# A streaming-encoder block on one core: the norm row loaded as one row and spread by two one-row products, and the opening's hand-written order rewritten up to the third tile

## The chip, the core and the metric

The kernel runs on one core of one Trainium2 chip. The core has a matrix engine (PE, whose weight loads the profile lists apart as PEld), a vector engine (DVE), a scalar engine (ACT), a general engine (POOL), and a sync engine (SP), which in this kernel does nothing but issue transfers. Each engine works through its own instructions in their order; an instruction waits for what it needs from other engines, and everything behind it on the same engine waits with it. Transfers run beside the engines.

The metric is the device time of one execution in microseconds (us). Before the change the median of three runs is 1209.71 us.

## The reference, cut to what matters

One block: a mixer with two branches, then a squared-ReLU MLP, for 1024 tokens of width 1024 and 16 meta tokens put ahead of them, all in float32.

```python
def rmsnorm(x, g):
    xf = x.astype(jnp.float32)
    y = xf * lax.rsqrt(jnp.mean(xf * xf, axis=-1, keepdims=True) + EPS)
    return (y * g.astype(jnp.float32)).astype(x.dtype)

def hybrid_mixer(u, w_in, ...):
    z = jnp.einsum('bld,dn->bln', u, w_in)
    a, q, k, v, r, lr, ga, gb = jnp.split(z, IN_SPLITS, axis=-1)
    ...
    return jnp.einsum('bld,de->ble', m, w_out)

def reference(x, meta_tokens, norm_mix, w_in, ...):
    meta = jnp.broadcast_to(meta_tokens[None].astype(x.dtype), (B, N_META, D_MODEL))
    h = jnp.concatenate([meta, x], axis=1)
    for l in range(DEPTH):                                  # DEPTH = 1
        h = h + hybrid_mixer(rmsnorm(h, norm_mix[l]), w_in[l], ...)
        h = h + squared_relu_mlp(rmsnorm(h, norm_ffn[l]), w_ff1[l], w_ff2[l])
    return rmsnorm(h, norm_final)[:, N_META:]
```

The change touches only the first line of the mixer: `rmsnorm(h, norm_mix[l])`, its transposes, and the first part of `u @ w_in`, the columns of `v` (512) and of `lr` (16).

## The kernel before, in words

The block is a row of stages. The change lies in the first, `first_stage`, and in the table `ORDER_1` that orders it. This stage takes the tokens in eight tiles of 128 and a ninth of the 16 meta tokens. For each tile it computes the norm, writes the normed tile, turns it by transposes (the channels must lie on the partitions for the products), and multiplies it with the columns of `w_in` for `v` and `lr`. The turned tiles stay in memory and serve all later stages.

**Precision.** PE multiplies float32 slowly, so nearly all products of the kernel are made with split operands: a matrix is held as a rounded part (`th`, `vw[:, 0]`, type fp32r) and the rest (`tl`, `vw[:, 1]`), and a product is three products (lines 285 to 287). ACT makes a rounded part by a copy, DVE the rest by a subtraction. The one exception is the first result, tile 0 with the first 256 columns: it is made in plain float32 from an unsplit copy `xr` of the turned tile (line 388), which doesn't have to wait for any splitting.

**The words of the order.** `ORDER_1` is a list of words, worked off one after the other when the program is written; ACT, DVE and SP keep this order as it stands (a manual schedule); PE's is left to a scheduler, which here leaves the turns and products in the order of the words. The first digit is the tile, or the number of the column block for words that deal with weights; the second is which half of the 1024 channels.

| word | engine | what it does | line before |
|---|---|---|---|
| `square t` | ACT | squares of the tile, summed per token, into a spare tile `um` | 488 |
| `log t`, `exp t` | ACT | first guess of the inverse root, by way of a logarithm | 491, 494 |
| `root t` | DVE | one Newton step on the guess, 3 small instructions | 498 to 500 |
| `scale t` | DVE | tile times root times norm row `gB`, into `us`; then issues a later tile's load on SP | 504 |
| `turn tj` | PE | 4 transposes 128x128 into a bank, `ms` and `sc` by turns | 519 |
| `keep tj` | ACT | copy of the turned half into `xr` | 525 |
| `hi tj`, `lo tj` | ACT, DVE | rounded part `th` and rest `tl` of the turned half | 532, 535 |
| `high ij`, `low ij` | ACT, DVE | rounded part and rest of weight block i, half j, into `vw`; i = 2 is the small `lr` block | 547, 551 |
| `ask ij` | SP | load of weight block i, half j, into a ring `raw` of two buffers (line 118), so it waits until the old block is used | 461 |
| `value itj` | PE | products of tile t, half j, with weight block i: 4 of plain float32 for the first two words, else 12 split ones | 388, 285 to 287 |
| `out it` | ACT | evacuates a finished result and stores it | 405 |

**Ahead of the words** stands a fixed opening. SP issues the loads of tiles 0 and 1, of the first two weight blocks, of tiles 2 and 3 and of the small `lr` block. ACT's queue issues the load of an identity matrix (`ident`, for the transposes), then the load of the norm row as 8 rows of 128 into eight partitions of a cleared 128x128 corner of `us`, and loads ACT's tables. PE runs two products 128x512 of a cleared buffer whose results nobody reads (`warm(2)`), then spreads the norm row over all partitions: eight products 128x128, each with one column of the identity, repeated, as its other operand, four into each of two banks (line 481). Three more warming products follow (`warm(3)`). DVE copies each of the two banks, times -0.5, into `gB` (line 484); the -0.5 belongs to the Newton step. Only then come the words.

Tile t is held in buffer t mod 4 of `xs`, and normed in buffer t mod 3 of `us`, so a tile's load or its scaling can wait for an earlier tile to be used up.

Of the kernel before, what the change touches and what calls it, by code (L numbers as in the profile page):

```python
# [10 lines left out]
ACT = mybir.ActivationFunctionType  # L11
ALU = mybir.AluOpType
AX = mybir.AxisListType

P = 128
# [3 lines left out]
KT = D // P  # L19
# [103 lines left out]
def kernel(  # L123
# [10 lines left out]
    act, dve, pool, pe = nc.scalar, nc.vector, nc.gpsimd, nc.tensor  # L134
# [19 lines left out]
    def bank(tag):  # L154
        if tag == "sc":
            sc_n[0] += 1
            return two("sc")[:, sc_n[0] % 2]
        return psp[tag].tile([P, 512], F32, name=f"b_{tag}", tag=tag)

    def two(tag):  # L160

        if tag in ("sc", "gs"):
            if tag not in wide:
                wide[tag] = psp[tag].tile([P, 2, 512], F32, name=f"b_{tag}", tag=tag)
            return wide[tag]
        return psp[tag].tile([P, 2, 512], F32, name=f"b_{tag}", tag=tag)
# [204 lines left out]
    def halves():  # L371
        return [slice(h * HALF, (h + 1) * HALF) for h in range(2)]
# [35 lines left out]
    def lr_turn():  # L408
# [13 lines left out]


    ORDER_1 = """
        square0 log0 exp0 root0 square1 scale0 log1 exp1 turn00 high00 root1 turn01 keep00 scale1 keep01 value000
        hi00 low00 ask10 high01 turn10 square2 low01 turn11 value001 ask11 hi10 log2 lo10 exp2 square3 root2 value010 scale2
        hi11 hi01 log3 lo11 out00 turn20 exp3 turn21 hi20 root3 value011 high10 lo20 scale3 high20 hi21 low20 value020 keep10
        keep11 lo01 square4 lo21 turn30 turn31 lo00 hi30 value021 log4 lo30 hi31 keep30 lo31 value030 exp4 keep20 out01
        root4 high11 low10 value031 out02 keep21 square5 scale4 value100 low11 wait00 log5 out03 exp5 turn40 turn41 root5
        value101 hi40 scale5 lo40 hi41 lo41 keep31 keep40 value110 out10 keep41 square6 log6 exp6 value111 value120  # L430
# [8 lines left out]
    def first_stage(xs, us, xm, um, lrraw):  # L439
        xr, vw = S["xr"], S["vw"]  # L440
        vraw = S["vraw"] = []
        x_in = lambda t: xs[:, t % 4] if t < 8 else xm
        x_out = lambda t: us[:, t % 3] if t < 8 else um[:META]
        tok = lambda t: (t // 4, OFF[t // 4] + (t % 4) * P)
        cell = lambda n, t: stat[n][: P if t < 8 else META, t : t + 1]

        def load(t):
            nc.sync.dma_start(xs[:, t % 4], x[t * P : (t + 1) * P, :])
# [2 lines left out]
            return w_in[4 * j * P : 4 * (j + 1) * P, c : c + n].rearrange("(k p) c -> p k c", p=P)  # L451

        blank = xr.rearrange("p k c -> p (k c)")[:, -640:]
        row = us[:, 2, :P]
        nc.scalar.dma_start(ident, ident_in)
        dve.memset(row, 0.0)
        nc.scalar.dma_start(row[:KT], norm_mix.rearrange("(k c) -> k c", c=P))
        act.preload_act_table_set("natural_log_exp_and_others")
        pool.memset(blank, 0.0)
        pool.memset(wgu, 0.0)  # L460
# [11 lines left out]
        def warm(n, cols=HALF):  # L472
            for _ in range(n):
                pe.matmul(bank("ms")[:, :cols], blank[:, HALF:], blank[:, :cols], start=True, stop=True)

        warm(2)
        for h, c in enumerate(halves()):
            b = bank("mm")
            for i in range(4):
                k = 4 * h + i  # L480
                pe.matmul(
                    b[:, i * P : (i + 1) * P], ident[:, k : k + 1].broadcast_to([P, P]), row, start=True, stop=True
                )
            dve.tensor_scalar(gB[:, c], b, -0.5, None, ALU.mult)
        warm(3)

        def square(t):
            act.activation(um[: P if t < 8 else META], x_in(t), ACT.Square, accum_out=cell(3, t))
# [13 lines left out]
        def scale(t):  # L502
            u = x_out(t)
            dve.scalar_tensor_tensor(u, x_in(t), cell(3, t), gB[: u.shape[0]], ALU.mult, ALU.mult)
            if t == 0:
                load(4)
            if t == 1:
                load(5)
                nc.sync.dma_start(xm, meta)
            if t in (2, 3):  # L510
                load(4 + t)

        turned = {}

# [34 lines left out]
        def low(i, j):  # L549
            whole, hi, lo = parts(i, j)  # L550
            dve.tensor_tensor(lo, whole, f32(hi), ALU.subtract)

        does = dict(
            wait=lambda i, j: W1.ask(),
            square=square, log=log, exp=exp, root=root, scale=scale, turn=turn, keep=keep, hi=hi, lo=lo, high=high,
            low=low, ask=ask, value=v_half, out=v_out, first=W1.split, meta=lambda t: transposed(um[:META], 0, 0),
        )
# [1181 lines left out]
```

## Time and profile before

| what | value |
|---|---|
| median of the runs | 1209.71 us |
| single runs | 1208.96, 1209.71, 1209.78 us |
| the profiled execution | 1210.91 us |
| its span (first to last instruction) | 1209.1 us |
| mean granted TensorE clock over it | 0.998 of full speed |
| busy DVE, ACT, POOL | 837.5, 574.4, 79.1 us |
| DMA, mean over the span | 159 GB/s |

The profile shows one execution. A row that begins with two numbers is a run of like instructions that follow each other on an engine: its start and its length in us from the span's start, then the engine, the line, the operation, result <- operands with their shapes, and `x` with the count; in square brackets stands how long the engine was idle just before, and what ended that. Rows of the busy time by stretches begin with start:end. Products on PE are pipelined, so that the length of one is not the distance to the next. The stage of the change takes about the first 74 us of the span; everything behind it is the same code in both kernels.

### The profile page before, as it was taken

What the parts mean: (1) busy time and instruction counts of PE and PEld (TensorE: products, weight loads), DVE (VectorE), ACT (ScalarE), POOL (GpSimd) and SP (SyncE); (2) the same over time, 40 slices, a digit from 0 to 9 for tenths busy, and PEclk for the clock granted to TensorE, in tenths of its full rate; (3) what the DMA queues carried; (4) which work ended last, traced back from release to release, by engine and by line L of the source; (5) the groups of instructions that cost most, each with busy time, mean ns of one, the idle gap of its engine ahead of it and who ended that gap; (6) DMA issues with size and microseconds to landing.
All of it is one profiled execution on the core that took longest, in us unless ns stands there. A gap on an engine that the chain in (4) does not pass through costs nothing.

```text
span 1209.1 us, 18303 instructions
## 1 busy us (share of the span) xinstructions
PE 1194.4 (99%) x6775; PEld 993.1 (82%) x6775; DVE 837.5 (69%) x1369; ACT 574.4 (48%) x1014; POOL 79.1 (7%) x97
## 2 busy tenths in 40 slices
PE   9999999999999999999999999999999999999997
PEld 7999877878778887788788888888888888888886
DVE  6636567565686669726887767677675887887686
ACT  7546444444456124305655545455464444444554
POOL 0000062323320000000000000000000000000000
PEclk9999999999999999999999999999999999999999
DMA  8223253534348978812255444444479963333532
GB/s 245 77 60 123 91 133 110 166 110 146 112 138 296 315 218 268 284 32 87 88 161 168 151 139 157 148 160 151 152 253 318 348 229 98 98 100 91 173 96 88
DMA packets 151385, 192.79 MB, mean 159 GB/s; under 512 B 12216, under 2 KB 86256, under 8 KB 151296
## 3 DMA queue, kind: packets, MB, share of 16 engines
q1 hardware_dynamic: 151136, 191.56, 49.5%
q8 instruction: 53, 0.87, 0.3%
q14 instruction: 36, 0.29, 0.1%
q10 hardware_dynamic: 160, 0.07, 0.0%
HBM read 128.66 MB, written 62.93 MB: 158 GB/s over the span
## 4 chain that ended last, share of the span: by engine, by line
PE 68%; DVE 3%; issue 1%; DMA 1%; ACT 1%; DVEq 0%; ACTq 0%
PE b_oa L287 5%; PE b_oa L285 5%; PE b_oa L286 5%; PE b_y L285 4%; PE b_y L286 4%; PE b_y L287 4%; PE b_mm L285 4%; PE b_mm L287 4%; PE b_mm L286 4%; PE b_ob L287 4%; PE b_ob L285 4%; PE b_ob L286 4%; PE b_z L286 3%; PE b_z L285 3%; PE b_z L287 3%; PE b_sc L285 2%
## 5 line engine op out<-in xcount | busy, mean ns | idle before, releaser
L774 ACT ACTIVATE w1h<-raw 128x512 fp32r<-128x512 f32 x106 | 65.8, 622 | 51.2 <-PE b_sc L286 21.2
L285 PE MATMUL b_sc<-th,w1h 128*128 128x512 f32 x216 | 85.4, 395 | 0.4 <-ACT u2p L1522 0.4
L285 PE MATMUL b_z<-th,w1h 128*128 128x512 f32 x216 | 84.9, 393 | 0.4 <-DVE c L893 0.4
L775 DVE TENSOR_TENSOR w1l<-raw,w1h 128x512 fp32r<-128x512 f32 x106 | 72.5, 685 | 18.0 <-ACT w1h L774 18.0
L286 PE MATMUL b_sc<-tl,w1h 128*128 128x512 f32 x216 | 84.8, 393 | 0.0
L286 PE MATMUL b_z<-tl,w1h 128*128 128x512 f32 x216 | 84.2, 390 | 0.4 <-DVE tl L1408 0.4
L287 PE MATMUL b_sc<-th,w1l 128*128 128x512 f32 x216 | 84.4, 391 | 0.0
L287 PE MATMUL b_z<-th,w1l 128*128 128x512 f32 x216 | 84.1, 389 | 0.0
L774 ACT ACTIVATE w1h<-fs 128x512 fp32r<-128x512 f32 x81 | 51.1, 630 | 67.0 <-PE b_y L286 33.6
L775 DVE TENSOR_TENSOR w1l<-fs,w1h 128x512 fp32r<-128x512 f32 x81 | 57.7, 712 | 23.7 <-ACT w1h L774 23.7
L285 PE MATMUL b_mm<-th,w1h 128*128 128x512 f32 (+1 forms) x208 | 72.0, 346 | 0.0
L287 PE MATMUL b_mm<-th,w1l 128*128 128x512 f32 (+1 forms) x208 | 71.1, 342 | 0.0
L286 PE MATMUL b_mm<-tl,w1h 128*128 128x512 f32 (+1 forms) x208 | 71.0, 342 | 0.0
L774 ACT ACTIVATE w1h<-bt 128x512 fp32r<-128x512 f32 x46 | 29.1, 632 | 70.8 <-issue 43.9
L1598 DVE TENSOR_TENSOR bt<-w,w 128x512 f32<-128x512 f32 x80 | 54.7, 683 | 2.7 <-DMA w<-in_w_ff_dram 2.7
L285 PE MATMUL b_mm<-wo,th 128*128 128x512 f32 x128 | 50.4, 394 | 0.9 <-PE b_mm L287 0.9
L287 PE MATMUL b_mm<-wo,tl 128*128 128x512 f32 x128 | 49.9, 390 | 0.0
L286 PE MATMUL b_mm<-wo,th 128*128 128x512 f32 x128 | 49.8, 389 | 0.0
L285 PE MATMUL b_y<-wo,w1h 128*128 128x512 f32 x128 | 49.8, 389 | 0.0
L286 PE MATMUL b_y<-wo,w1h 128*128 128x512 f32 x128 | 49.8, 389 | 0.0
L287 PE MATMUL b_y<-wo,w1l 128*128 128x512 f32 x128 | 49.8, 389 | 0.0
L775 DVE TENSOR_TENSOR w1l<-bt,w1h 128x512 fp32r<-128x512 f32 x46 | 31.8, 691 | 25.6 <-ACT w1h L774 25.6
(425 smaller groups left out, 3317.1 us busy)
## 6 DMA issues: line engine op xcount, KB each, us to landing
hf_dram<-h SPq DMA_DIRECT2D x112, 256.0 KB, 2.1
raw<-hf_dram SPq DMA_DIRECT2D x112, 256.0 KB, 2.6
w<-in_w_ff_dram SPq DMA_DIRECT2D x64, 256.0 KB, 4.8
raw<-in_w_in_dram SPq DMA_DIRECT2D x22, 512.0 KB, 4.7
raw<-in_w_ff_dram SPq DMA_DIRECT2D x16, 512.0 KB, 4.1
rawx<-in_w_ff_dram SPq DMA_DIRECT2D x16, 512.0 KB, 4.1
rawp<-in_w_in_dram SPq DMA_DIRECT2D x10, 512.0 KB, 4.2
xs<-in_x_dram SPq DMA_DIRECT2D x8, 512.0 KB, 4.8
```

The source lines that it names most:

```text
L285: pe.matmul(ps, ah, bh, start=first and i == 0, stop=False, skip_group_check=more)
L286: pe.matmul(ps, ah, bl, start=False, stop=False, skip_group_check=more)
L287: pe.matmul(ps, al, bh, start=False, stop=last and i == n - 1, skip_group_check=more)
L774: act.activation(hi, a, ACT.Copy)
L775: dve.tensor_tensor(lo, a, f32(hi), ALU.subtract)
L1598: dve.tensor_tensor(bt, w, S["w2"][q[3:]][:, i], ALU.add if q[2] == "+" else ALU.subtract)
```

## The change

The norm row is loaded as one row of 1024 into one partition, as the first transfer that SP issues. Two products with a row of ones, each 512 wide with a single row to sum over (`spread0`, `spread1`), put it on all partitions; DVE copies the first bank (`copy0`), ACT the second (`copy1`). One warming product 512 wide stands ahead of them instead of two, and three of 128 columns behind them instead of three of 512. Tile 0 is scaled in two halves of 512 channels (`half0`, `half1`), of which the second issues the load of tile 4. The table of words is new up to `hi01`; from `lo20` on the two lists read alike; every word of the old list other than `scale0` is still there once. Behind the change lines shift: what was line 488 to 504 is 491 to 507, `half` is 516, `turn` 526, `keep` 532, `hi` 539, `lo` 542, `high` 554, `low` 558, and the copies of `gB` are 486 (ACT) and 488 (DVE).

```diff
--- before.py
+++ after.py
@@ -422,9 +422,9 @@
 
 
     ORDER_1 = """
-        square0 log0 exp0 root0 square1 scale0 log1 exp1 turn00 high00 root1 turn01 keep00 scale1 keep01 value000
...
+        spread0 spread1 warm3 copy0 square0 log0 exp0 root0 copy1 half0 half1 square1 log1 exp1 turn00 turn01 keep00 root1 keep01
...
         keep11 lo01 square4 lo21 turn30 turn31 lo00 hi30 value021 log4 lo30 hi31 keep30 lo31 value030 exp4 keep20 out01
         root4 high11 low10 value031 out02 keep21 square5 scale4 value100 low11 wait00 log5 out03 exp5 turn40 turn41 root5
         value101 hi40 scale5 lo40 hi41 lo41 keep31 keep40 value110 out10 keep41 square6 log6 exp6 value111 value120
@@ -451,10 +451,10 @@
             return w_in[4 * j * P : 4 * (j + 1) * P, c : c + n].rearrange("(k p) c -> p k c", p=P)
 
         blank = xr.rearrange("p k c -> p (k c)")[:, -640:]
-        row = us[:, 2, :P]
+        row, ones = us[:1, 2], us[:1, 1, :P]
         nc.scalar.dma_start(ident, ident_in)
-        dve.memset(row, 0.0)
-        nc.scalar.dma_start(row[:KT], norm_mix.rearrange("(k c) -> k c", c=P))
+        dve.memset(ones, 1.0)
+        nc.sync.dma_start(row, norm_mix[None, :])
         act.preload_act_table_set("natural_log_exp_and_others")
         pool.memset(blank, 0.0)
         pool.memset(wgu, 0.0)
@@ -473,16 +473,19 @@
             for _ in range(n):
                 pe.matmul(bank("ms")[:, :cols], blank[:, HALF:], blank[:, :cols], start=True, stop=True)
 
-        warm(2)
-        for h, c in enumerate(halves()):
-            b = bank("mm")
-            for i in range(4):
-                k = 4 * h + i
-                pe.matmul(
-                    b[:, i * P : (i + 1) * P], ident[:, k : k + 1].broadcast_to([P, P]), row, start=True, stop=True
-                )
-            dve.tensor_scalar(gB[:, c], b, -0.5, None, ALU.mult)
-        warm(3)
+        warm(1)
+        rows = []
+
+        def spread(h):
+            rows.append(bank("mm"))
+            pe.matmul(rows[h], ones, row[:, halves()[h]], start=True, stop=True)
+
+        def copy(h):
+            c = halves()[h]
+            if h:
+                act.activation(gB[:, c], rows[h], ACT.Copy, scale=-0.5)
+            else:
+                dve.tensor_scalar(gB[:, c], rows[h], -0.5, None, ALU.mult)
 
         def square(t):
             act.activation(um[: P if t < 8 else META], x_in(t), ACT.Square, accum_out=cell(3, t))
@@ -502,14 +505,18 @@
         def scale(t):
             u = x_out(t)
             dve.scalar_tensor_tensor(u, x_in(t), cell(3, t), gB[: u.shape[0]], ALU.mult, ALU.mult)
-            if t == 0:
-                load(4)
             if t == 1:
                 load(5)
                 nc.sync.dma_start(xm, meta)
             if t in (2, 3):
                 load(4 + t)
 
+        def half(h):
+            c = halves()[h]
+            dve.scalar_tensor_tensor(x_out(0)[:, c], x_in(0)[:, c], cell(3, 0), gB[:, c], ALU.mult, ALU.mult)
+            if h:
+                load(4)
+
         turned = {}
 
         def turn(t, j):
@@ -551,6 +558,7 @@
             dve.tensor_tensor(lo, whole, f32(hi), ALU.subtract)
 
         does = dict(
+            spread=spread, copy=copy, half=half, warm=lambda n: warm(n, P),
             wait=lambda i, j: W1.ask(),
             square=square, log=log, exp=exp, root=root, scale=scale, turn=turn, keep=keep, hi=hi, lo=lo, high=high,
             low=low, ask=ask, value=v_half, out=v_out, first=W1.split, meta=lambda t: transposed(um[:META], 0, 0),
```

Three places on the engines show what moves. The first is ACT's start, from its first square on. `um,small<-xs` is a square, the two 128x1 rows behind it log and exp, `gB<-b_mm` the new copy, `xr<-b_` a keep, `vw_186<-raw_` a `high` of the first weight block, `th_132<-b_` a `hi`. Before:

```order
L488 ACTIVATE um,small<-xs 128x1024
L491 ACTIVATE small<-small 128x1
L494 ACTIVATE small<-small 128x1
L488 ACTIVATE um,small<-xs 128x1024
...
L547 ACTIVATE vw_186<-raw_116 128x1024
L525 ACTIVATE xr<-b_sc 128x4x128
L525 ACTIVATE xr<-b_ms 128x4x128
L532 ACTIVATE th_132<-xr 128x4x128
L547 ACTIVATE vw_186<-raw_120 128x1024
```

After the change:

```order
L491 ACTIVATE um,small<-xs 128x1024
L494 ACTIVATE small<-small 128x1
L497 ACTIVATE small<-small 128x1
L486 ACTIVATE gB<-b_mm 128x512
...
L532 ACTIVATE xr<-b_sc 128x4x128
L532 ACTIVATE xr<-b_ms 128x4x128
L554 ACTIVATE vw_186<-raw_116 128x1024
L491 ACTIVATE um,small<-xs 128x1024
L539 ACTIVATE th_132<-b_sc 128x4x128
L539 ACTIVATE th_132<-b_ms 128x4x128
L554 ACTIVATE vw_186<-raw_120 128x1024
```

The copy of `gB` is new between the first exp and the second square; `high00` (`raw_116`) moved from ahead of the two keeps of tile 0 to behind them, and `high01` (`raw_120`) from behind `hi00` to behind the third square and both halves of tile 1 (`hi10`, `hi11`).

The second place is ACT around `out00` (the row `vo<-b_mm`), where tile 2 is turned. `th_132<-b_` are the halves of tiles 1 and 2, `th_132<-xr` those of tile 0, `vw_190` is the second weight block. Before:

```order
L532 ACTIVATE th_132<-b_ms 128x4x128
L532 ACTIVATE th_132<-xr 128x4x128
L491 ACTIVATE small<-small 128x1
L405 ACTIVATE vo<-b_mm 128x256
L494 ACTIVATE small<-small 128x1
L532 ACTIVATE th_132<-b_sc 128x4x128
L547 ACTIVATE vw_190<-raw_116 128x4x256
L547 ACTIVATE vw_190<-lrraw 128x8x16
```

After the change:

```order
L539 ACTIVATE th_132<-xr 128x4x128
L494 ACTIVATE small<-small 128x1
L405 ACTIVATE vo<-b_mm 128x256
L497 ACTIVATE small<-small 128x1
L539 ACTIVATE th_132<-b_sc 128x4x128
L554 ACTIVATE vw_190<-raw_116 128x4x256
L539 ACTIVATE th_132<-xr 128x4x128
L554 ACTIVATE vw_190<-lrraw 128x8x16
```

Before, the first two rows are `hi11` and `hi01`; now the first is `hi00`, and `hi01` has gone behind `hi20` (the row from `b_sc`) and `high10`.

The third place is DVE between the scaling of tile 1 and that of tile 2 (the row with `gB`). `vw_186` are the two `low` of the first weight block, `tl_136` the rests of tile 1, the 128x1 rows `root2`. Before:

```order
L551 TENSOR_TENSOR vw_186<-raw_116,vw_186 128x1024
L551 TENSOR_TENSOR vw_186<-raw_120,vw_186 128x1024
L535 TENSOR_TENSOR tl_136<-b_sc,th_132 128x4x128
L498 TENSOR_SCALAR small<-small 128x1
...
L504 SCALAR_TENSOR_TENSOR us<-xs,small,gB 128x1024
L535 TENSOR_TENSOR tl_136<-b_ms,th_132 128x4x128
```

After the change:

```order
L558 TENSOR_TENSOR vw_186<-raw_116,vw_186 128x1024
L542 TENSOR_TENSOR tl_136<-b_sc,th_132 128x4x128
L542 TENSOR_TENSOR tl_136<-b_ms,th_132 128x4x128
L558 TENSOR_TENSOR vw_186<-raw_120,vw_186 128x1024
L501 TENSOR_SCALAR small<-small 128x1
...
L507 SCALAR_TENSOR_TENSOR us<-xs,small,gB 128x1024
```

Both rests of tile 1 now stand between the two `low`, and the scaling of tile 2 stands directly behind `low01` and `root2`.

More of the change, by code (lines that the diff above doesn't have):

```diff
@@ L424 @@
     ORDER_1 = """
-        square0 log0 exp0 root0 square1 scale0 log1 exp1 turn00 high00 root1 turn01 keep00 scale1 keep01 value000
-        hi00 low00 ask10 high01 turn10 square2 low01 turn11 value001 ask11 hi10 log2 lo10 exp2 square3 root2 value010 scale2
-        hi11 hi01 log3 lo11 out00 turn20 exp3 turn21 hi20 root3 value011 high10 lo20 scale3 high20 hi21 low20 value020 keep10
+        spread0 spread1 warm3 copy0 square0 log0 exp0 root0 copy1 half0 half1 square1 log1 exp1 turn00 turn01 keep00 root1 keep01
+        high00 scale1 value000 low00 square2 turn10 turn11 hi10 hi11 lo10 value001 ask10 high01 lo11 log2 exp2 low01
+        value010 ask11 root2 scale2 square3 hi00 value011 log3 out00 turn20 exp3 turn21 hi20 root3 high10 hi01 lo20 scale3 high20 hi21 low20 value020 keep10
         keep11 lo01 square4 lo21 turn30 turn31 lo00 hi30 value021 log4 lo30 hi31 keep30 lo31 value030 exp4 keep20 out01
```

## The prediction

> **What bounds the kernel now.** I read the page first, then the busy time by stretches, then the first 25 us instruction by instruction. The change touches nothing behind the first stage.
>
> ```profile
> PE 1194.4 (99%) x6775; PEld 993.1 (82%) x6775; DVE 837.5 (69%) x1369; ACT 574.4 (48%) x1014; POOL 79.1 (7%) x97
> ...
> 1.46 3.78 PE L474 MATMUL b_ms<-xr 128*128 128x512 f32 x4 [1.46 <-POOL xr L459]
> 5.23 2.79 PE L481 MATMUL b_mm<-us,ident 128*128 128x128 f32 x16
> 7.86 2.74 PE L474 MATMUL b_ms<-xr 128*128 128x512 f32 x6
> 10.71 0.66 PE L519 MATMUL b_sc<-ident,us 128*128 128x128 f32 x4
> ...
> 12.05 1.13 PE L388 MATMUL b_mm<-raw,xr 128*128 128x256 f32 x4 [0.25 <-ACT xr L525]
> ```
>
> PE is busy 99% of the span, but what it does before 12.05 us (warming, spreading, transposes) is preparation: the first product of the result starts at 12.05. From there every instruction of PE is needed, so a change here gains only as much as the last stall of PE comes earlier. What sets 12.05 is a chain through DVE:
>
> ```profile
> 7.17 0.69 DVE L484 TENSOR_SCALAR gB<-b_mm 128x512 f32<-128x512 f32 x1 [6.14 <-PE b_mm L481]
> 8.06 0.69 DVE L484 TENSOR_SCALAR gB<-b_mm 128x512 f32<-128x512 f32 x1 [0.20 <-PE b_mm L481]
> ...
> 8.93 0.22 DVE L499 SCALAR_TENSOR_TENSOR small<-small 128x1 f32<-128x1 f32 x1
> 9.37 1.28 DVE L504 SCALAR_TENSOR_TENSOR us<-xs,small,gB 128x1024 f32<-128x1024 f32 x1
> ...
> 16.12 0.14 DVE L498 TENSOR_SCALAR small<-small 128x1 f32<-128x1 f32 x1
> 16.81 1.28 DVE L504 SCALAR_TENSOR_TENSOR us<-xs,small,gB 128x1024 f32<-128x1024 f32 x1
> ```
>
> The norm row arrives only in time for 5.23, its spreading ends near 8.0, two copies follow (7.17 and 8.06), then the root (its second step at 8.93) and the scaling of tile 0 (9.37 to 10.65); turn00 is at 10.71. A second view says what happens to any lead won there:
>
> ```profile
> 12.00:18.00 6.00, 5.95 (x36) 5.35 (x36) 5.24 (x8) 5.97 (x13) 0.00 (x0) 1.00 0.83 243
> 18.00:24.00 6.00, 5.92 (x52) 5.85 (x52) 5.31 (x12) 5.64 (x14) 0.00 (x0) 1.00 0.91 283
> 24.00:30.00 6.00, 6.00 (x52) 5.96 (x51) 5.69 (x12) 5.91 (x16) 1.24 (x1) 1.00 0.62 138
> 30.00:40.00 10.00, 10.00 (x84) 10.00 (x83) 5.95 (x12) 6.94 (x16) 0.00 (x0) 1.00 0.48 142
> ```
>
> The columns are length, then busy time of PE, its weight loads, DVE and ACT. From 12 to 30 us ACT is busy 5.97, 5.64 and 5.91 of 6, DVE 5.24 to 5.69: they are as full as PE and feed it step by step. Only after 30 us (6.94 and 5.95 of 10) do they have room. So the change is worth the lead that ACT and DVE, not PE, still have near 24 us, where PE last depends on them closely.
>
> **The change part by part.** *Row load.* It leaves ACT's queue and becomes SP's first load, so every other early load of SP is issued one step later.
>
> ```profile
> 0.75 0.86 SPq L448 DMA_DIRECT2D xs<-in_x_dram  x2
> ...
> ident<-in_ident_dram ACTq DMA_DIRECT2D x1, 64.0 KB, 4.1
> ...
> wgu<-in_w_gate_up_dram SPq DMA_DIRECT2D x1, 16.0 KB, 1.8
> ```
>
> Two issues take 0.86 us, so a step is about 0.43 us. When the row lands is not shown: the nearest small load took 1.8 us (so 2.6), the ident load, in the same microsecond as the big ones, 4.1 (so 4.9). I take about 2.9, nearer to the small load, as nothing is queued ahead of it. Up to 3.3 it costs nothing, since the one warming product (half of 3.78 us) covers it.
>
> *Spreading.* 16 instructions (2.79 us) and one warming product before them go; two products 128x512 come, and three short warming products behind them, which lie in PE's wait for the first half tile (until 8.1) and cost nothing. ACT's queue loses an issue ahead of its table load, all before tile 0 lands (4.68): nothing either. At the slow pace of the first row a product is 1.89 us, 1.71 apart as they overlap: 1.46 + 3.78 + 1.71 = 6.95 us for the end of the second, against 8.0.
>
> *ACT.* Its steps:
>
> ```profile
> 4.68 1.06 ACT L488 ACTIVATE um<-xs 128x1024 f32<-128x1024 f32 x1 [1.59 <-DMA xs<-in_x_dram]
> 6.25 0.20 ACT L494 ACTIVATE small<-small 128x1 f32<-128x1 f32 x1
> 6.36 1.04 ACT L488 ACTIVATE um<-xs 128x1024 f32<-128x1024 f32 x1
> 7.52 0.29 ACT L491 ACTIVATE small<-small 128x1 f32<-128x1 f32 x1
> ...
> 7.96 1.04 ACT L547 ACTIVATE vw<-raw 128x1024 fp32r<-128x1024 f32 x1
> 11.40 0.60 ACT L525 ACTIVATE xr<-b_sc 128x512 f32<-128x512 f32 x1 [2.40 <-PE b_sc L519]
> 11.90 0.59 ACT L525 ACTIVATE xr<-b_ms 128x512 f32<-128x512 f32 x1
> 12.38 0.63 ACT L532 ACTIVATE th<-xr 128x512 fp32r<-128x512 f32 x1
> 12.89 1.06 ACT L547 ACTIVATE vw<-raw 128x1024 fp32r<-128x1024 f32 x1
> 13.84 1.05 ACT L488 ACTIVATE um<-xs 128x1024 f32<-128x1024 f32 x1
> 14.88 0.59 ACT L532 ACTIVATE th<-b_sc 128x512 fp32r<-128x512 f32 x1
> ```
>
> Start to start, a square before its log takes 1.16, log and exp 0.44 (7.52 to 7.96), a 128x512 copy 0.48 to 0.50, a `high` 0.95, a square alone 1.04. With tile 0 landing 0.43 later, exp0 ends at 6.45 + 0.43 = 6.88. The new copy1, of keep00's shape, must wait for the second product: 7.00. Behind it queue square1 at 7.50, log1 8.66, keep00 9.10, keep01 9.60, high00 10.08, square2 11.03. DVE meanwhile makes copy0 (5.3), root0 (its step at 8.93 is the one that needs exp0, and the scaling came 0.44 behind it: 6.93 + 0.44 = 7.37), and the halves (about 0.69 each, by the 128x512 copies at 7.17 and 8.06; half of 1.28 if less) end at 8.1 and 8.8. The second half needs copy1, done at 7.6: no wait. turn00 runs at 8.15 to 8.8, keep00 at 9.10, and the first product starts at 9.75: **2.30 us earlier** than 12.05. keep00 now waits for ACT's queue, not for PE.
>
> *The order to the third tile.* The distance from the first product to turn10 was 13.88 - 12.05 = 1.83, so turn10 is at 11.58 and done at 12.18.
>
> ```profile
> 13.88 0.60 PE L519 MATMUL b_sc<-ident,us 128*128 128x128 f32 x4
> ...
> 13.98 1.23 DVE L551 TENSOR_TENSOR vw<-raw,vw 128x1024 fp32r<-128x1024 f32 x1 [0.29 <-ACT vw L547]
> 14.08 2.98 SPq L118 DMA_DIRECT2D raw<-in_w_in_dram  x2
> ...
> 18.15 0.66 PE L519 MATMUL b_sc<-ident,us 128*128 128x128 f32 x4
> ...
> 18.84 0.60 ACT L532 ACTIVATE th<-b_sc 128x512 fp32r<-128x512 f32 x1 [0.36 <-PE b_sc L519]
> 19.43 1.06 ACT L547 ACTIVATE vw<-raw 128x1024 fp32r<-128x1024 f32 x1
> ```
>
> ACT goes on: hi10 12.2, hi11 12.7, high01 13.16, which ends at 14.22. DVE's low01 can start then (14.27), and the new order puts root2 and scale2 behind it: low01 ends at 15.5, root2 to scale2 is 16.81 - 16.12 = 0.69, scale2 runs 16.1 to 17.4, turn20 17.45, hi20 18.14. Before, turn20 was at 18.15 and hi20 at 18.84. Of the lead of 2.30 us **0.70 is left**. The rest goes on ACT: between keep01 and high01, where only hi00 stood, it now makes high00, square2, hi10 and hi11 (0.95 + 1.04 + 0.48 + 0.48), so high01 comes at 13.16 against 12.89, not earlier at all; only lo10, now done ahead of low01 on DVE, still brings scale2 forward. ACT in turn has square3, hi00, log3, out00 and exp3 done near 16.7 and then stands idle some 1.4 us for turn20. On PE value010 and value011 (12 instructions of 0.12 each) are moved together and end near 17.0: it stalls 0.45 too.
>
> Behind hi20 come high10 and, new at this place, hi01 (0.48, which stood ahead of hi20); high10 no longer waits for its load: 18.84 + 0.48 = 19.32 against 19.43 are 0.11, and the load's issue (14.08) waits for the first products and low00, which now end near 11.7 and 12.4. So hi21 and all that follows on ACT, in the old order, is 0.70 + 0.11 - 0.48 = **0.33 us earlier**. PE has to take that pace where it needs tile 3:
>
> ```profile
> 23.71 0.69 DVE L535 TENSOR_TENSOR tl<-b_sc,th 128x512 fp32r<-128x512 f32 x1 [0.34 <-ACT th L532]
> ...
> 24.34 0.28 PE L286 MATMUL b_mm<-vw,th 128*128 128x256 f32 x1
> 24.45 0.39 PE L287 MATMUL b_mm<-vw,tl 128*128 128x256 f32 x1
> 24.68 0.28 PE L285 MATMUL b_mm<-vw,th 128*128 128x256 f32 x1
> ```
>
> lo30 ended at 24.40 and the product that needs it ran at 24.45, the next 0.23 later instead of 0.12: even before, PE arrived just in time. Now it arrives early and waits until 24.12. Some 2.0 us of new stalls of PE between 17 and 24 us take the rest. Sum: 0.33 of 2.30 us remain. Span 1209.1 - 0.3 = 1208.8. The profiled execution took 1210.91 us, 1.8 more than its span; the median of the runs, 1209.71, is 1.2 under that, and I subtract from the median: **1209.4 us**.
>
> **Rivals.** *The whole lead is kept* (0.10): if ACT and DVE had room, all 2.30 us stay, 1207.4. For it: the stall before 12.05 is PE's last longer one. Against it: 5.97 of 6 busy.
>
> *The clock stays slow* (0.11), the other side. The same product cost 0.94 us an instruction at 1.46 (3.78 / 4) and 0.46 at 7.86 (2.74 / 6). Before, PE warmed without a hole until 10.6; now it works on one row of 128 and has holes (about 7.4 to 8.15, 9.4 to 9.75). If the slow pace lasts through the first four products and the eight transposes behind them, they take 1.7 + 0.5 longer; PE had 0.45 to spare before turn20 (17.0 against 17.45), so turn20 is 1.75 later and the result 1.4 slower: 1211.1; through value001 too, 1212.8. It decides from a delay of 0.8 us on (0.45 and the 0.33).
> The Trainium skill, "TensorE: Matmul & The Clock Gate", Part 1 ("What's actually happening"), has the gate open after a busy window of about 3.4 us and close after an idle one; Part 4 says that transposes do not count as busy work in the same way. By that, 7.4 to 9.75 would be a hole of 2.4 us, shorter than a window, so the gate would stay open and 1209.4 would stand; but it bears on why I give this rival more than a trifle.
>
> *The row lands late* (0.10): at 5.2 as before, the four instructions end near 7.9 instead of 6.95, ACT is 0.9 later throughout, and 0.3 of gain turns into 0.6 of loss: 1210.3. That the change would not do what it says I leave out: the order on the engines shows it.
>
> **How the numbers follow.** Forecast 0.69, rivals 0.10, 0.11, 0.10. The forecast's own range is 1208.8 to 1210.2: the slack of single steps, and the row up to its late end. The range, 1207.8 to 1211.0, takes in the late row and the near half of the kept lead and of the slow clock, leaving out about 0.18. A measurement of this kernel tells 0.2%, 2.4 us, from no change. Faster by that needs more than the whole lead: 0.03. Slower needs the long case of the slow clock: 0.05. Same: 0.92.
>
> **What would show it.** Right: the first product of `b_mm<-raw,xr` near 9.75; ACT idle more than 1 us before hi20 near 18.1; stalls of PE that wait for DVE's `tl` and `us` between 17 and 24; lo30's product at 24.1. Wrong: the first product after 10.5 (late row or slow clock, told apart by the duration of the two spreading products and the transposes), or PE without stalls until 24 us (lead kept).

## The result: 0.13% slower

The changed kernel takes 1211.11 us (median of 22 runs, 1210.14 to 1214.30) where the kernel before, run beside it, takes 1209.78 us (22 runs, 1208.96 to 1211.47). The ratio is 1.0013, with a 95% interval of 1.0007 to 1.0019: slower by 0.8 to 2.3 us. The forecast was 1209.4 us, a little faster, with a range up to 1211.0: the time lies 0.1 us outside the range, and there is a loss where a small gain was forecast.

The profiled execution has a span of 1210.4 us, 1.3 more than before. The rows that answer to those shown in the prediction are these: PE's first 25 us, in order of time (start, length, engine, line, operation, idle time ahead and what ended it).

```profile
1.46 2.07 PE L474 MATMUL b_ms<-xr 128*128 128x512 f32 x2 [1.46 <-POOL xr L459]
3.46 3.78 PE L481 MATMUL b_mm<-us 1*128 1x512 f32 x4
7.17 1.65 PE L474 MATMUL b_ms<-xr 128*128 128x128 f32 x6
8.61 1.06 PE L526 MATMUL b_sc<-ident,us 128*128 128x128 f32 x4
9.47 1.06 PE L526 MATMUL b_ms<-ident,us 128*128 128x128 f32 x4
10.36 3.45 PE L388 MATMUL b_mm<-raw,xr 128*128 128x256 f32 x8
13.65 0.60 PE L526 MATMUL b_sc<-ident,us 128*128 128x128 f32 x4
...
19.53 0.66 PE L526 MATMUL b_sc<-ident,us 128*128 128x128 f32 x4 [0.28 <-DVE us L507]
...
23.51 0.66 PE L526 MATMUL b_sc<-ident,us 128*128 128x128 f32 x4 [0.47 <-ACT xr L532]
```

The early row does come early: the spreading starts at 3.46, against 5.23 before. But four transposes take 1.06 us at 8.61 and 0.60 at 13.65, and the first eight value instructions take 3.45 us, where the kernel before needed 1.99 for the same: PE runs at half its pace until about 13.3 us. Where the text speaks of PE's clock, it means this pace, at which one and the same instruction takes either a certain time or half of it. Before, it doubled its pace at 6.9, within the spreading, where seven instructions from 5.79 on take 1.45 us and ten from 6.65 on 1.38:

```profile
5.79 1.45 PE L481 MATMUL b_mm<-us,ident 128*128 128x128 f32 x7
...
6.65 1.38 PE L481 MATMUL b_mm<-us,ident 128*128 128x128 f32 x10
...
12.05 1.99 PE L388 MATMUL b_mm<-raw,xr 128*128 128x256 f32 x8 [0.25 <-ACT xr L525]
```

So of a first product that is 1.69 us earlier (10.36 against 12.05) 0.23 is left at turn10 (13.65 against 13.88). From turn10 to turn20 another 1.6 is lost: 5.88 us lie between them, 4.27 before, and turn20 comes 1.38 us later than before. What lies between shows in the rows of ACT and DVE after the change:

```profile
14.29 0.60 ACT L539 ACTIVATE th<-b_sc 128x512 fp32r<-128x512 f32 x1 [1.14 <-PE b_sc L526]
14.78 0.59 ACT L539 ACTIVATE th<-b_ms 128x512 fp32r<-128x512 f32 x1
15.26 1.06 ACT L554 ACTIVATE vw<-raw 128x1024 fp32r<-128x1024 f32 x1
16.35 1.23 DVE L558 TENSOR_TENSOR vw<-raw,vw 128x1024 fp32r<-128x1024 f32 x1
17.49 0.14 DVE L501 TENSOR_SCALAR small<-small 128x1 f32<-128x1 f32 x1
18.19 1.28 DVE L507 SCALAR_TENSOR_TENSOR us<-xs,small,gB 128x1024 f32<-128x1024 f32 x1
...
20.22 0.60 ACT L539 ACTIVATE th<-b_sc 128x512 fp32r<-128x512 f32 x1 [1.38 <-PE b_sc L526]
```

This is a chain: ACT waits 1.14 us for turn10, makes hi10 and hi11, then high01; DVE's low01 waits for high01, and root2 and scale2 stand behind low01; turn20 waits for scale2. In the old order high01 stood ahead of hi10 and did not wait for turn10. Busy time by stretches (length, then busy PE, weight loads, DVE, ACT, POOL, granted clock, DMA share, GB/s) shows the same as idleness:

```profile
12.00:18.00 6.00, 6.00 (x37) 5.43 (x36) 4.02 (x7) 4.82 (x11) 0.00 (x0) 1.00 0.76 250
18.00:24.00 6.00, 4.77 (x35) 3.93 (x34) 5.03 (x10) 4.62 (x12) 0.00 (x0) 1.00 0.86 207
```

ACT, 5.97 of 6 us busy before in the first stretch, is now busy 4.82, and PE stands still for 1.23 of 6 us in the second. The column with the granted clock says 1.00 in both, though PE works at half its pace for the first 1.3 us of the first: that column does not show this; the lengths of like instructions do.

### The profile page after: what moved, and what is told of

It reads as the page before. It is cut to its first block, busy times and chain, and to the rows that moved or that the text cites. A ratio compares the mean times of both kernels' runs of the same rounds, so it can differ in the third digit from the quotient of the medians.

```text
span 1210.4 us, 18277 instructions
## 1 busy us (share of the span) xinstructions
PE 1195.3 (99%) x6761; PEld 993.4 (82%) x6761; DVE 837.0 (69%) x1369; ACT 575.2 (48%) x1015; POOL 78.0 (6%) x97
## 4 chain that ended last, share of the span: by engine, by line
PE 68%; DVE 3%; DMA 1%; issue 1%; ACT 1%; SPq 0%; DVEq 0%
PE b_oa L287 5%; PE b_oa L286 5%; PE b_oa L285 5%; PE b_y L285 4%; PE b_y L287 4%; PE b_y L286 4%; PE b_mm L285 4%; PE b_mm L287 4%; PE b_mm L286 4%; PE b_ob L287 4%; PE b_ob L286 4%; PE b_ob L285 4%; PE b_z L285 3%; PE b_z L286 3%; PE b_z L287 3%; PE b_sc L285 2%
```

## The experiments

The table has one profiled execution of each kernel: when PE doubled its pace (read from the distances of its instructions, to about 0.2 us), the start of the first value product, of turn10 and turn20 (tiles 1 and 2) and of the last product with `vw`, which ends the stage, and the medians. All experiments compute the whole result. The kernel before, run beside them, took 1209.90 us with the first eight and 1210.67, on another chip, with the last three; where those three are set beside others, their ratios count. What lies behind the stage is the same code in all of them and took between 1135.1 and 1137.6 us in the thirteen profiles, so that a difference at the end of the stage and one of the medians need not agree to better than about a microsecond.

| kernel | pace doubles | first value | turn10 | turn20 | end of stage | median us | ratio to before (95%) |
|---|---|---|---|---|---|---|---|
| before | 6.9 | 12.05 | 13.88 | 18.15 | 72.89 | 1209.78 | |
| changed | 13.3 | 10.36 | 13.65 | 19.53 | 74.69 | 1211.11 | 1.0013 (1.0007, 1.0019) |
| 1 full rows | 7.5 | 9.72 | 11.55 | 17.44 | 72.60 | 1209.82 | 1.0000 (0.9991, 1.0009) |
| 2 old order | 13.0 | 10.36 | 13.51 | 17.77 | 72.41 | 1209.76 | 1.0000 (0.9991, 1.0009) |
| 3 old opening, new order | 6.7 | 12.05 | 13.88 | 19.76 | 74.92 | 1211.81 | 1.0015 (1.0007, 1.0024) |
| 4 full rows, old order | 4.7 | 9.27 | 11.10 | 16.55 | 71.16 | 1208.52 | 0.9989 (0.9980, 0.9998) |
| 5 before, warming on one row | 11.2 | 13.95 | 15.78 | 20.05 | 74.68 | 1211.53 | 1.0013 (1.0004, 1.0022) |
| 6 full rows, hi01 back | 4.9 | 9.14 | 10.97 | 16.93 | 71.56 | 1209.06 | 0.9993 (0.9984, 1.0002) |
| 7 as 4, nothing split | 6.4, halves 9.8, doubles 13.1 | 10.93 | 13.83 | 18.34 | 72.96 | 1209.84 | 1.0000 (0.9991, 1.0009) |
| 8 as changed, 32 rows | 10.3 | 10.36 | 12.19 | 18.19 | 73.30 | 1210.61 | 1.0008 (0.9999, 1.0017) |
| 9 as 7, longer warming | 4.6 | 9.85 | 11.68 | 16.89 | 71.67 | 1209.48 | 0.9988 (0.9979, 0.9997) |
| 10 as 4, another order | 6.4 | 9.44 | 11.27 | 16.20 | 71.14 | 1208.39 | 0.9982 (0.9973, 0.9991) |
| 11 as 4, again | 7.1 | 9.72 | 11.55 | 16.76 | 71.42 | 1208.82 | 0.9984 (0.9975, 0.9993) |

Two theories were set against each other. A: what sets PE's clock does not count products on one row as work, so the change starts its clock late. C: the new order loses by itself, whatever the clock. Both turned out to be true, with about equal shares.

**1. Full rows.** The norm row goes to the last partition, the other 127 are zeroed, and the two products run over all 128; their result is the same.

```diff
-        row, ones = us[:1, 2], us[:1, 1, :P]
+        row, ones, rest = us[P - 1 :, 2], us[:, 1, :P], us[: P - 1, 2]
+        dve.memset(rest, 0.0)
...
-            pe.matmul(rows[h], ones, row[:, halves()[h]], start=True, stop=True)
+            pe.matmul(rows[h], ones, us[:, 2, halves()[h]], start=True, stop=True)
```

> The changed kernel, with the two spreading products over all 128 partitions (the norm row on the last one, zeros on the other 127) in place of one row; nothing else differs. Theory A (products on one row are not counted as work by what sets PE's clock, and this late clock is what the change loses by): the clock doubles near 7 us as before the change, in place of 13.3; first value product near 9.7, turn20 near 17.4, time 0.3 us under the kernel before (about 1209.5). Rival B (the clock stays slow because of the 128-column products and transposes behind the spreading, or by chance): doubles near 13 again, turn20 at 19.5, about 1211.1. Rival C (the new order loses by itself, whatever the clock): the clock doubles early, but the time stays over 1210.5.

PE's rows of this run:

```profile
3.33 3.62 PE L482 MATMUL b_mm<-us 128*128 128x512 f32 x4
6.75 1.21 PE L475 MATMUL b_ms<-xr 128*128 128x128 f32 x6
7.99 0.66 PE L527 MATMUL b_sc<-ident,us 128*128 128x128 f32 x4
...
9.72 1.99 PE L388 MATMUL b_mm<-raw,xr 128*128 128x256 f32 x8 [0.35 <-ACT xr L533]
11.55 0.60 PE L527 MATMUL b_sc<-ident,us 128*128 128x128 f32 x4
...
17.44 0.66 PE L527 MATMUL b_sc<-ident,us 128*128 128x128 f32 x4 [0.27 <-DVE small L502]
...
21.42 0.66 PE L527 MATMUL b_sc<-ident,us 128*128 128x128 f32 x4 [0.47 <-ACT xr L533]
```

The pace doubles near 7.5, during the same short warming products in which it stayed low before, the first value product starts at 9.72 and the eight take 1.99 us again. Everything behind lies where the forecast had it (9.75, 11.58, 17.45). The time goes from 1.3 us over the kernel before to level with it. So the number of rows of two products decided the clock, and the late clock costs 1.3 us here (1211.11 against 1209.82). But the kernel is not faster than before. C was set down with a time over 1210.5 us and did not come to that here; whether the new order loses by itself the second and the third experiment show.

**2. Old order.** The changed opening, one-row products included, and the old words behind value000.

```diff
-        high00 scale1 value000 low00 square2 turn10 turn11 hi10 hi11 lo10 value001 ask10 high01 lo11 log2 exp2 low01
+        high00 scale1 value000
+        hi00 low00 ask10 high01 turn10 square2 low01 turn11 value001 ask11 hi10 log2 lo10 exp2 square3 root2 value010 scale2
...
```

> The changed kernel's opening up to value000, one-row products included, with the old order of words behind it (hi00, low00, ask10, high01, turn10 and so on). The clock should double near 13.3 as in the changed kernel. If the loss needs the new order (which puts hi10 and hi11 between turn10 and high01, so that low01 and scale2 wait for turn10), scale2 no longer waits for turn10: turn20 near 17.5, time 0.3 us under the kernel before. If the slow clock costs by itself, in any order: turn20 after 18.9, time at least 0.7 us over the kernel before.

```profile
10.36 3.30 PE L388 MATMUL b_mm<-raw,xr 128*128 128x256 f32 x8
13.51 0.60 PE L527 MATMUL b_sc<-ident,us 128*128 128x128 f32 x4
...
17.77 0.66 PE L527 MATMUL b_sc<-ident,us 128*128 128x128 f32 x4
```

The clock is as late as in the changed kernel (the eight instructions take 3.30 us), turn10 comes at nearly the same time (13.51 against 13.65), and still turn20 is at 17.77 in place of 19.53 and the loss is gone. The old order has high01 made while PE crawls through value000 (from 12.53 on), and low01 follows at 13.60; the new one lets them wait for turn10 (15.26 and 16.35).

**3. Old opening, new order.** The kernel before, with the new words behind value000.

> The kernel before with its own opening up to value000, and the new order of words behind it. The clock doubles near 6.9 as before. If the new order ties turn20 to turn10 at a distance of 5.9 us (4.3 in the old order): turn10 at 13.8, turn20 at 19.7, time 2.0 us over the kernel before at the end of the stage, so 1211.3 to 1211.8. If only the late clock made the change slow: within 0.4 us of the kernel before.

```profile
13.88 0.60 PE L519 MATMUL b_sc<-ident,us 128*128 128x128 f32 x4
...
19.76 0.66 PE L519 MATMUL b_sc<-ident,us 128*128 128x128 f32 x4 [0.27 <-DVE small L498]
```

With turn10 exactly where it was, turn20 is 1.61 us later, and the kernel 1.9 us slower: the new order loses without any change of the clock. From turn10 to turn20 it takes 5.88 us here, 5.89 in the first experiment, 5.88 in the changed kernel, whatever the clock had done before (5.96 and 6.00 in the sixth and the eighth, which have the new order too). Which of the moved words costs how much was not tried one by one, hi01 in the sixth experiment excepted; that high01 is the link is read from the trace.

**4. Full rows, old order.** Both put right.

> The changed kernel's opening with the spreading products on 128 rows, and the old order of words behind value000. If theory A holds and the old order passes on more of the lead: first value product near 9.7, turn20 near 16.8, turn30 near 20.5, time 1.3 us under the kernel before (about 1208.5). If the clock stays slow: like the changed opening with the old order, 0.3 us under it. If the lead is lost behind tile 3 in any order: 0 to 0.4 us under it.

```profile
7.92 0.66 PE L528 MATMUL b_sc<-ident,us 128*128 128x128 f32 x4 [1.41 <-DVE us L518]
...
9.27 1.99 PE L388 MATMUL b_mm<-raw,xr 128*128 128x256 f32 x8
11.10 0.60 PE L528 MATMUL b_sc<-ident,us 128*128 128x128 f32 x4
...
16.55 0.66 PE L528 MATMUL b_sc<-ident,us 128*128 128x128 f32 x4 [0.46 <-DVE us L509]
```

1208.52 us, 1.4 under the kernel before, interval clear of no change. So the four corners add up: the late clock costs 1.2 to 1.3 us in either order (1209.76 to 1208.52, 1211.11 to 1209.82), the new order 1.3 to 1.4 with either clock (1209.82 to 1208.52, 1211.11 to 1209.76; behind the old opening, in the third experiment, 1.9), and the new opening with full rows and the old order brings 1.4. With one row and the old order it brings nothing that can be told from zero (the second experiment). PE doubled its pace earlier than expected here (4.7), and so the first value product is at 9.27 in place of 9.7 and turn20 at 16.55 in place of 16.8.

**5. Before, with its first warming on one row.** A tested from the other side: the first four instructions of the kernel before, whose results nobody reads, run on one row.

```diff
-        def warm(n, cols=HALF):
+        def warm(n, cols=HALF, r=P):
...
-                pe.matmul(bank("ms")[:, :cols], blank[:, HALF:], blank[:, :cols], start=True, stop=True)
-
-        warm(2)
+                pe.matmul(bank("ms")[:, :cols], blank[:r, HALF:], blank[:r, :cols], start=True, stop=True)
+
+        warm(2, r=1)
```

> The kernel before, with its first two warming products (four instructions, 1.46 to 5.24 us) on one row instead of 128; nothing else differs, and nobody reads their results. Theory A (products on one row don't count for what sets PE's clock): the clock can only start counting at 5.2, so it doubles 3.2 to 6 us later, between 8.4 and 11.2, in place of 6.9; the spreading and the warming behind it run at half pace, turn00 moves from 10.7 to 12 or 13, turn20 from 18.2 to 19.5 or 20.4, time 1.4 to 2.3 us over the kernel before. Rival: any product counts: the clock doubles near 6.9, time unchanged.

```profile
1.46 3.78 PE L474 MATMUL b_ms<-xr 1*128 1x512 f32 x4 [1.46 <-POOL xr L459]
5.49 3.75 PE L481 MATMUL b_mm<-us,ident 128*128 128x128 f32 x16 [0.25 <-DMA us<-in_norm_mix_dram]
9.03 3.80 PE L474 MATMUL b_ms<-xr 128*128 128x512 f32 x6
12.66 0.60 PE L519 MATMUL b_sc<-ident,us 128*128 128x128 f32 x4
```

The four instructions take the 3.78 us that they took on 128 rows, but the pace doubles only at 11.2 in place of 6.9; the sixteen spreading instructions take 3.75 us (2.79 before), and turn00 is 1.95 us later. The loss, 1.6 us, lies within what theory A expected, and the rival (any product counts) is out.

**6. One word back.** The first experiment with hi01 behind hi00 again.

```diff
-        value010 ask11 root2 scale2 square3 hi00 value011 log3 out00 turn20 exp3 turn21 hi20 root3 high10 hi01 lo20 scale3 high20 hi21 low20 value020 keep10
+        value010 ask11 root2 scale2 square3 hi00 hi01 value011 log3 out00 turn20 exp3 turn21 hi20 root3 high10 lo20 scale3 high20 hi21 low20 value020 keep10
...
```

> The kernel with full-row spreading and the new order (the first experiment), with one word put back: hi01 directly behind hi00, where ACT waits for turn20 anyway, in place of behind high10. By the prediction's step (its 0.48 us on ACT stand ahead of hi21 and all that follows): turn20 unchanged at 17.4, turn30 0.5 us earlier, time 0.5 us under the first experiment and 0.9 under the kernel before. If that word costs nothing: time as in the first experiment.

```profile
16.93 0.66 PE L527 MATMUL b_sc<-ident,us 128*128 128x128 f32 x4 [0.32 <-DVE small L502]
...
20.39 0.66 PE L527 MATMUL b_sc<-ident,us 128*128 128x128 f32 x4
```

From turn20 to turn30 it takes 3.46 us, 3.98 in the first experiment (17.44 to 21.42): 0.52 for one ACT copy of 0.48. Turn20 did not stay at 17.4, since the pace doubled at 4.9 in this profile and turn10 was 0.58 earlier; the distance of turn20 to it is 5.96, 5.89 in the first experiment. By the medians the kernel is 0.8 us under the first experiment, of which the profile gives 0.5 to the word; the intervals of the two overlap, so that the times alone do not show it.

**7. Nothing split.** The fourth experiment with both banks copied by DVE and tile 0 scaled in one piece.

```diff
-        spread0 spread1 warm3 copy0 square0 log0 exp0 root0 copy1 half0 half1 square1 log1 exp1 turn00 turn01 keep00 root1 keep01
...
+        spread0 spread1 warm3 copy0 copy1 square0 log0 exp0 root0 square1 scale0 log1 exp1 turn00 turn01 keep00 root1 keep01
...
```

> The kernel with full-row spreading and the old order (the fourth experiment), with both banks of the norm row copied by DVE and tile 0 scaled in one piece, as before the change. If splitting this work brings most of the lead: turn00 at 9.2 to 9.5 in place of 7.9, turn20 near 17.8, time 1.1 us over the fourth experiment, 0.3 under the kernel before. If the early row alone brings it: within 0.3 us of the fourth experiment.

```profile
6.52 0.83 PE L476 MATMUL b_ms<-xr 128*128 128x128 f32 x6
9.39 0.85 PE L527 MATMUL b_sc<-ident,us 128*128 128x128 f32 x4 [2.03 <-DVE small L500]
10.03 1.06 PE L527 MATMUL b_ms<-ident,us 128*128 128x128 f32 x4
10.93 3.06 PE L388 MATMUL b_mm<-raw,xr 128*128 128x256 f32 x8
13.83 0.60 PE L527 MATMUL b_sc<-ident,us 128*128 128x128 f32 x4
```

The time came out near the expectation (1.3 over the fourth, 1.1 expected), but not for the reason given. PE doubled its pace at 6.4, stood still for 2.03 us while DVE made the root and scaled the whole tile (8.05 to 9.33; the row names the small instruction that DVE had begun by then), and halved it again at 9.8, in the middle of turn00; it doubled once more at 13.1. So the price measured here may be mostly that of the clock, and the splitting is not yet measured; the ninth experiment separates the two.

**8. 32 rows.** The changed kernel with the spreading products on 32 rows, 31 of them zeros.

> The changed kernel with the two spreading products on 32 rows (31 of them zeros), in place of one row or 128. If what sets the clock weighs a product by the rows it uses: the clock doubles near 13 as with one row, about 1211.1. If it counts any product on more than one row as work: it doubles near 7, as in the first experiment, and the time is about that of the kernel before.

```profile
9.47 0.97 PE L527 MATMUL b_ms<-ident,us 128*128 128x128 f32 x4
10.36 1.99 PE L388 MATMUL b_mm<-raw,xr 128*128 128x256 f32 x8
```

It came out between the two expectations: the pace doubles at 10.3, 3.1 us after the first of the unbroken full-row products (7.17), and the kernel takes 1210.61 us. In the kernels that warm on full rows from 1.46 on it doubles by 7.5 at the latest, so that 32 rows did not count as 128 do. Whether they count for nothing or for a part, one profile does not say; the times leave it open too, as the interval of the ratio (0.9999 to 1.0017) takes in both the 1.0013 of the changed kernel and the 1.0000 of the first experiment.

**9. Nothing split, longer warming.** The seventh with the hole filled: the three products behind the spreading are 384 columns wide.

> The seventh experiment (full-row spreading, old order, tile 0 scaled in one piece, both copies on DVE) with the three short warming products made 384 columns wide instead of 128, so that PE has no hole of 2 us before turn00. In the seventh, the clock doubled near 6.4, fell back near 9.8 behind a hole of PE from 7.4 to 9.4, and doubled again near 13. If the hole made it fall back: the clock stays up from 7 us on, turn00 near 9.4, turn10 near 12.4, turn20 near 17.8, 0.2 to 0.3 us under the kernel before; and what the splitting of copies and scaling is worth by itself is then its distance to the fourth experiment, 1.1 us. If the hole was not the cause: the clock falls back again near 10, and the time is that of the seventh.

```profile
5.54 2.10 PE L476 MATMUL b_ms<-xr 128*128 128x384 f32 x6
8.50 0.66 PE L527 MATMUL b_sc<-ident,us 128*128 128x128 f32 x4 [0.86 <-DVE small L500]
9.00 0.60 PE L527 MATMUL b_ms<-ident,us 128*128 128x128 f32 x4
9.85 1.99 PE L388 MATMUL b_mm<-raw,xr 128*128 128x256 f32 x8 [0.25 <-ACT xr L533]
```

The hole is 0.86 us, the pace stays up, and the stage ends 1.3 us earlier than in the seventh: by this the hole was the cause, as far as one profile of each can say; the times agree (ratio 0.9988 to the kernel before, in place of 1.0000). The turns lie 0.7 to 0.9 us earlier than expected, as the pace doubled at 4.6 already. What is left to the splitting is 0.7 us by the medians (1209.48 against 1208.82 of the eleventh, beside it on the same chip; the intervals overlap). By the end of the stage it is 0.25 against the eleventh (71.42), whose pace doubled at 7.1, and 0.51 against the fourth (71.16), whose pace doubled at 4.7, nearly as here. 1.1 was expected.

**10 and 11. Another order, and the fourth once more.** This order is meant to leave ACT and DVE idle for as little as possible. It is one long line in the kernel, broken here; up to value011 it reads

```text
spread0 spread1 warm3 copy0 square0 log0 exp0 root0 copy1 half0 half1 square1 turn00 log1 exp1 turn01 keep00 root1
scale1 high00 hi00 keep01 value000 turn10 low00 high01 value001 ask10 low01 ask11 hi10 turn11 square2 log2 exp2 lo10
square3 hi11 value010 hi01 root2 scale2 turn20 log3 exp3 lo11 out00 hi20 root3 lo20 turn21 scale3 high10 value011 ...
```

> Full-row spreading and the split opening (the fourth experiment) with another order up to scale3, in which scale1 and high00 come earlier, hi10 stands ahead of square2, and root2 and scale2 directly behind lo10. If DVE and ACT have room left: turn20 near 16.3, 0.3 us earlier than in the fourth experiment, time 0.3 us under it (about 1208.2). If they don't: time as in the fourth experiment.

> The fourth experiment once more, beside the two before it on the same chip: 1.2 to 1.5 us under the kernel before. PE's clock can double at another time in it (4.7 us there), which should move nothing behind turn10 as long as it comes before 8 us.

The fourth repeats (ratio 0.9984 here, 0.9989 there). The other order has turn20 0.56 us earlier and the end of the stage 0.28 earlier, and a median 0.4 lower (1208.39 against 1208.82), but the intervals of the two overlap almost wholly: that it is better is not shown. Both are faster than the kernel before, run beside them.

## Why the prediction was wrong, point by point

**The likeliest case took the wrong clock.** The step that failed is the one that put the first product at 9.75 and turn10 another 1.83 us behind it, at 11.58: it took PE's pace of before for granted. The runs showed 10.36 for the first product and 3.29 us from there to turn10 (13.65), as the pace doubled only at 13.3; with the same two products on full rows it doubled at 7.5, and the two were 9.72 and 1.83. The prediction weighed a slow clock, named the reason ("now it works on one row of 128 and has holes"), and gave it 0.11. It was the first half of that reason. The holes were not there at all: PE was busy from 1.46 to the end of value000. The prediction's sentences on the Trainium skill asked whether a gate that is open would close in a hole; here the pace had not doubled yet, and whether products on one row bring the doubling nearer was the question to ask. The sign set down for a slow clock, a first product after 10.5, would have missed it too, at 10.36; the length of the transposes shows it (1.06 us in place of 0.60).

**That rival's price came out right, to the hundredth by luck.** Written for this case were 1211.1 us, with turn20 at 17.45 + 1.75 = 19.20. Measured: 1211.11, with turn20 at 19.53. The delay itself was nearly right: 2.07 us at turn10 (13.65 against 11.58), for 1.7 + 0.5. But the slack of 0.45 that was taken off is not there: turn20 is late by the same amount (19.53 against 17.45, 2.08). It was the slack of PE's products, and turn20 hangs on turn10 through ACT and DVE, by the prediction's own steps. At the end of the stage 1.80 us are lost (74.69 against 72.89), of 1.4 written; the span shows 1.3, so that 0.5 came back behind the stage, which differs by as much between profiles anyway. The range stopped at half of that case, and so missed by 0.1 us. Its remark that only 2.4 us can be told from no change was too wide: with 22 runs of each kernel, 1.3 was told.

**The small terms held, within 0.3 us.** Tile 0's first square starts at 5.06 (4.68 + 0.43 was assumed); copy1 ends at 7.88 and the halves at 8.06 and 8.73, for 7.6, 8.1 and 8.8. The row is there for the spreading, which waits for no transfer worth naming (3.33 in the first experiment, right behind the warming). The spreading ends at 7.24 in place of 6.95.

**The distances in the new order held.** From turn10 to turn20: 5.87 forecast, 5.88 to 5.89 measured in three kernels, 5.96 and 6.00 in two. With the clock mended (experiment 1) the lead at turn20 is 0.71, for 0.70 forecast, and at the end of the stage 0.29, for 0.33; and hi01 costs 0.52 for 0.48. The sum of the likeliest case, 0.3 us under the kernel before, is thus what the first experiment shows in its stage; its median, 0.1 under, cannot tell that from nothing.

**What was explained wrongly is why the lead shrinks.** The prediction put it down to ACT and DVE having no room between 12 and 30 us, and read the worth of the opening from that. The first experiment and the eleventh differ in the order alone, and in both the first value product is at 9.72 and turn10 at 11.55. The new order keeps 0.71 us of lead at turn20 and 0.29 at the end of the stage, the old one 1.39 and 1.47. The stretch from 12 to 18 us reads, in the first and in the eleventh:

```profile
12.00:18.00 6.00, 5.74 (x43) 5.32 (x42) 5.04 (x11) 4.67 (x13) 0.00 (x0) 1.00 0.94 286
12.00:18.00 6.00, 5.32 (x37) 4.54 (x36) 5.04 (x11) 5.60 (x15) 0.00 (x0) 1.00 1.07 317
```

In the new order ACT is busy for only 4.67 us of 6: it has room and stands waiting in the chain. The loss of 1.3 us is the new order's, in which hi10 and hi11 wait for turn10, high01 stands behind them, and low01 and scale2 behind that. In the old order ACT is busy for 5.60 us and comes to hi10 only at 13.50, 1.35 us after turn10 is done: there the prediction's reason holds, and it may be what takes the 0.9 us between the lead of 2.33 at the first product and that of 1.47. The prediction's own steps had the chain (high01 "not earlier at all"), but it never set the old order beside the new one with the early opening; the runs put 1.3 us between them.

**The other rivals.** The whole lead was not kept in any kernel; of 2.8 us at the first product, experiment 4 kept 1.7. The row was not late.

## What to carry to other kernels

When a small product replaces large ones at a program's start, ask not only how long it takes but whether PE doubles its pace as early as before: filling the unused rows with zeros cost PE no time and here saved 1.3 us. A reordering and an earlier start are two changes: measure each alone, since here the earlier start, on full rows, gained 1.4 us and the new order lost as much. And a high busy share before a change doesn't show what will be the limit after it; a distance between two events that stays the same when the first one moves (turn10 to turn20 in the new order, 5.88 to 6.00 in five kernels) points to a chain.

## What the runs showed of the hardware that was not expected

**Rows count for the clock.** Products on one row take the time of those on 128 (3.78 us for four instructions either way) but did not bring the doubling of PE's pace nearer. In the nine profiles in which all products from 1.46 us on worked on full rows, the doubling came 3.1 to 6.0 us later. In the four others it came 3.1 to 6.1 us after the first unbroken full-row work (7.17 in the changed kernel, the second and the eighth experiment, 5.49 in the fifth).

**In one trace the pace changed in steps of about 3.3 us, and the moment of the first doubling changes from execution to execution.** In the seventh experiment it doubled at 6.4, halved at 9.8 and doubled at 13.1. The same code doubled at 4.7 in one profile and at 7.1 in the other (experiments 4 and 11). The Trainium skill, "TensorE: Matmul & The Clock Gate", Part 1 ("What's actually happening"), describes a free-running window of about 3.4 us, and these steps agree with it. That the 22 times of the changed kernel spread more than those of the kernel before (4.2 us against 2.5) may come from the moment of the doubling; it was not tested.

**A hole of 2.03 us went with a halving of the pace in the one profile that has it (experiment 7)**, while holes of 1.41 us (experiment 4) and 0.86 us (experiment 9) did not. The Trainium skill, "TensorE: Matmul & The Clock Gate", under "Why this matters for your kernels", warns of idle gaps over some 3 us; the measured one is shorter, and the measurement decides.
